# A hybrid conv and attention layer: a fifth weight group in seven products, conv taps by ScalarE and adding DMAs

## The chip, the cores and the metric

The kernel runs on one core of one Trainium2 chip. The metric is the device time of one execution in microseconds, the median of several. TensorE (PE) does matrix products, VectorE (DVE) and ScalarE (ACT) work on whole tiles, GpSimd (POOL) does small scalar work here and issues the DMAs that add to their destination, SyncE (SP) issues most other DMAs. Each engine works through its own instructions in the order in which the program issues them.

## The reference

One decoder layer on x of 512 tokens by 2048 channels, in float32:

```python
h = rms_norm(x, norm_g)
z = h @ w_in                                  # 2048 x 7168
a_val, a_glu, a_gate, q, k, v, b_gate = split(z, 7 x 1024)

u = a_val * sigmoid(a_glu)
u = causal_depthwise_conv(u, conv_w, conv_b)  # 31 taps, 1024 channels
u = silu(layer_norm(u, conv_norm_g, conv_norm_b))
y_a = (u @ conv_pw_w + conv_pw_b) * silu(a_gate)

q, k = rms_norm(q), rms_norm(k)               # per head, 16 heads of 64
o = dilated_attention_mixture(q, k, v)        # three causal patterns, mixed
y_b = o * silu(b_gate)

out = x + concat(y_a, y_b) @ w_out            # 2048 x 2048
```

## The kernel before, in words

**Units, groups, slots.** Weights come in groups of 512 output columns; a group of w_in has four *units* of 4 x 128 rows (1 MB each). The list GROUPS sets the order: four "vg" groups (value and gate of the GLU), q0, k0, v0, bg0 (half of the b-gate), q1, k1, v1, ag0, ag1, bg1, then w_out and pointwise groups ("wb", "pw", "wc", "wa"). A unit is eight *slots* of TensorE work; `clock[0]` counts slots, and everything else is placed by slot: `after(n, fn)` puts a step n slots ahead into `calendar`, and each slot first issues its due steps, then its matmuls. So the order on every engine is written out by hand through the many step constants (IN_HI, NORM, B_STEPS, WA_PARTS and so on).

**Precision.** A float32 product is made of three float16 ones: each operand is split into a high and a low part (`split_hi`/`hi` on ScalarE, `split_lo`/`lo` on VectorE), and `tri` issues high x high, high x low, low x high. The scale of a group comes from a bound on its weights: `measure` sums squares on ScalarE, `bound` adds them up through TensorE, VectorE and POOL. The first two groups are done in float32 matmuls (`exact_matmuls`), while the sums for the RMS norm of x are still being made.

**Seven products.** The groups in SEVEN (before: vg3, q0, k0, v0) use a scheme of seven half-size block products instead of eight (`input_products`): sums of weight blocks are made in place by adding DMAs on POOL's queue and one difference on VectorE, sums of x blocks are made once (`sum_x`), and the results are joined in `copy`, `joint`, `fourth` and `out`. Such a group has 28 steps instead of 32 slots. The "wa" groups of w_out use the same scheme (`seven_products`, `seven_parts`).

**The weight ring.** `raw_pool` has eight 1 MB buffers. When a unit's low part is made, its buffer is let go, the unit eight further on is loaded, and some slots later it is measured.

**Conv.** `conv` is a generator that works through channel blocks 0 to 7 in pairs. A block's 31 taps are one ScalarE instruction (with the bias) and 30 multiply-adds on VectorE, each over up to 512 tokens. `run_conv` pulls taps from it each slot while an estimate of VectorE's load lies below PACE, a number of nanoseconds for each slot. After the last pair come the sums for the layer norm, the norm itself and the split of its result into `u16`, which the "pw" units read.

**Attention.** `attention(hf)` places pairs of heads at fixed slots (`at_pair`), PERIOD slots apart: scores at 0 and 3, exps, reciprocal roots, high and low parts, a transposing DMA (`turn`), and then `values` and `put` in `end_pair`, which the next pair's `begin` calls, or the last pair's own step.

Of the kernel before, what the change touches and what calls it, by code (L numbers as in the profile page):

```python
# [19 lines left out]
P = 128  # L20
# [13 lines left out]
WARM = 9  # L34
KU = 4
PERIOD = {0: 32, 1: 32}
# [3 lines left out]
PACE_FROM = (63, 114, 169, 225, 297, 361)  # L40
PACE = [1170, 1350, 1285, 1310, 1480, 1465, 1480]
# [8 lines left out]
GROUPS = [("vg", 0), ("vg", 1), ("vg", 2), ("vg", 3), ("q", 0), ("k", 0), ("v", 0), ("bg", 0), ("q", 1), ("k", 1), ("v", 1),  # L50
# [12 lines left out]
B0_AT = -13  # L63
YB = [0, 1, 4, -2, -1, 3]
B_STEPS = [-5, 3, 20, 7]
B1_STEPS = [3, 9, 28, 6]
Y_STEPS = [5, 1]
Y_SUMS = [2, 1, 2, 1]
SPLIT_PW = [0, 2]
# [4 lines left out]
NORM = {'q': [3, 8, 8, 10, 5], 'k': [3, 7, 9, 13, 5]}  # L74
NORM_K0 = [3, 1, 10, 11, 13, 2]
WA_ADD = [{'s1': (4,), 's4': (1,), 's2': (-4,), 's3': (-8,)}, {'s1': (8, 9, 14), 's4': (2, 3, 8), 's2': (-2, -1, 4), 's3': (-10, -9, -9)}, {'s1': (8, 9, 12), 's4': (2, 3, 8), 's2': (-2, -1, 4), 's3': (-16, -15, -16)}, {'s1': (5, 6), 's4': (0, 2), 's2': (-3, -2), 's3': (-16, -15)}]
WA_PARTS = [{'a11': (-29,), 'a22': (-27,), 'a12': (-1,), 's3': (1,), 's2': (4,), 's1': (7,), 's4': (9,)}, {'a11': (-8, -7, -3), 'a22': (-4, -3, 2), 'a12': (-2, 2, 5), 's3': (4, 5, 10), 's2': (8, 9, 14), 's1': (11, 12, 17), 's4': (15, 16, 21)}, {'a11': (-7, -7, -2), 'a22': (-4, -3, 2), 'a12': (-1, 0, 5), 's3': (4, 5, 10), 's2': (8, 9, 14), 's1': (11, 12, 17), 's4': (15, 16, 21)}, {'a11': (-5, -5), 'a22': (-4, -3), 'a12': (-2, -1), 's3': (0, 1), 's2': (4, 5), 's1': (7, 8), 's4': (10, 11)}]
WA_OUT = [1, 4, 1, 5, 5, 6, 6]
MEASURE = 16
BOUND = [3, -3, 6, 5]  # L80
SPLIT_AT = [0, 3]
MEASURE_AT = [15, 9]
# [27 lines left out]
def layer(ctx: ExitStack, tc: tile.TileContext, xt, w1, w2, w3, g_in, conv_w, conv_b,  # L110
# [45 lines left out]
    A.activation(small.tile([P, 1], F32, name="warm", bufs=1), ones[:, 0:1], AF.Copy)  # L156
# [156 lines left out]
    def exact_hi(n):  # L313

        i, k = divmod(n, KU)
        wt = parts[i, k] = part_pool.tile([P, 2, S], R32, name="wr", tag="part")
        A.activation(wt[:, 0], raw[i][:, k], AF.Copy)

    def exact_lo(n):
# [3 lines left out]
        if k == KU - 1:  # L323
            raw.pop(i)
            load(i + RING)
            after(max(6, 32 - 3 * i - 5 * (8 - RING)), lambda: measure(i + RING))
# [9 lines left out]
    def split_lo(i):  # L336
        if i < n_plain:
            wh, wl = parts[i]
            V.scalar_tensor_tensor(wl, raw.pop(i), wscale[units[i][3:]][0], wh, op0=OP.mult, op1=OP.subtract)
            load(i + RING)  # L340
            after(MEASURE_AT[of_next(i) not in SEVEN], lambda: measure(i + RING))

# [15 lines left out]
    def split_x(k):  # L358
# [10 lines left out]
        A.activation(h, x, AF.Copy, scale=g)  # L369
# [97 lines left out]
    def evac_vg(g, m, ps):  # L467
# [15 lines left out]
        elif m % 2 == 0:  # L483
            t = glu[i] = temp("glu")
            if g < FIRST:
# [4 lines left out]
        else:  # L490
            t = u[i] = slot("u")
            if g < FIRST:
                V.tensor_mul(t, ps, rrow)
                V.tensor_mul(t, t, glu.pop(i))
# [99 lines left out]

    def shifted():
# [5 lines left out]
        for i in range(6):  # L601
            square(i)
            yield
            if len(squares) > 1:
                V.tensor_add(acc2[0], acc2[0], squares.pop(0))
                yield
        V.tensor_add(acc2[0], acc2[0], squares.pop(0))

    def conv():

        for i0 in range(0, 8, 2):
            while i0 + 1 not in u:
                yield 1
            for i in (i0, i0 + 1):
                cv[i] = slot("cv")
                A.activation(cv[i], u[i], AF.Identity, scale=cw[:, i, TAPS - 1:TAPS], bias=cb[:, i:i + 1])  # L616
            yield 2
            for j in range(TAPS - 2, -1, -1):
# [9 lines left out]
            elif i0 == 2:  # L628
                for i in (i0, i0 + 1):
                    nc.gpsimd.dma_start(acc, cv[i], accum_op=OP.add)  # L630
            elif i0 == 4:
                for i in (i0, i0 + 1):
                    V.tensor_add(acc, acc, cv[i])
                    yield 0
# [30 lines left out]
        for i in range(8 + 2):  # L665
# [9 lines left out]
            yield LN_STEPS[7]  # L675

# [125 lines left out]
    def two_heads(pair):  # L802
# [78 lines left out]
        for a, e in ((0, 7), (1, 11)):  # L881
            h = (13, 18)[a]
            plan += [(6, lambda a=a: shift(a)), (e + 4, lambda a=a: roots(a)), (h + 6, lambda a=a: turn(a))]
            for i in range(NT):
                plan += [(e, lambda a=a, i=i: exps(a, i))]
                plan += [(h + i // 2, lambda a=a, i=i: high(a, i)), (h + 3 + i // 2, lambda a=a, i=i: low(a, i))]
# [9 lines left out]
    def attention(hf):  # L896
        start = max(clock[0] + 28, max(at_pair.values(), default=0) + PERIOD[0])
        start += (PHASE - start) % 8
        for p4 in range(4):
            at_pair[4 * hf + p4] = start + p4 * PERIOD[hf]  # L900

            def begin(pair=4 * hf + p4):
                end_pair(pair - 1)
# [7 lines left out]
                after(PERIOD[hf] - (pair == 7), lambda: end_pair(pair))  # L911
# [104 lines left out]
    def seven_parts(g):  # L1016
# [182 lines left out]
    def input_products(i0):  # L1199
# [20 lines left out]
        def lo(name, pair):  # L1220
# [61 lines left out]
        def out(name):  # L1282
# [19 lines left out]
            elif kind == "v":  # L1302
# [5 lines left out]
                after(2, lambda: V.tensor_tensor(to[:, :, :, DH:], src, to[:, :, :, :DH], op=OP.subtract))  # L1308
            else:
# [37 lines left out]
    for k in range(2):  # L1347
        load_part(0, k, k + 1)
        fetch_x(k)
    for n in range(1, 8):  # L1350
# [6 lines left out]
    for n in range(2):  # L1357
        exact_hi(n)
        exact_lo(n)
        split_x(n)  # L1360
    exact_hi(2)
# [3 lines left out]
    def startup(n):  # L1365
# [8 lines left out]
        if n == 0:  # L1374
# [7 lines left out]
            for m in (32, 33, 36):  # L1382
# [158 lines left out]
```

## Time and profile before

| | |
|---|---|
| median of 3 runs | 811.38 us (811.3 to 811.81) |
| profiled execution | 810.59 us, span 808.8 us |
| TensorE busy | 802.1 us (99%) |
| VectorE busy | 718.1 us (89%) |
| ScalarE busy | 571.4 us (71%) |
| POOL busy | 161.2 us (20%) |
| DMA queues | SP and ACT 42.8%, POOL 15.3% of 16 engines |

The span runs from the first to the last instruction. Busy times are sums over an engine's instructions. A row of a group of instructions names line, engine, operation, output<-inputs and shapes, the count, then busy us and mean ns of one, and the idle time of the engine ahead of it with what ended it. A row of the waits has engine and instruction, what it waited for, the total, the number of times and the longest. Nearly all VectorE instructions have line 105, the helper that records their load.

### The profile page before, as it was taken

The page shows a single profiled execution, that of the slowest core. Times are in us where ns is not written, and L with a number is a line of the kernel's source. Part 1 is how long each engine was busy: PE and PEld are TensorE (multiplying, and loading weights), DVE is VectorE, ACT ScalarE, POOL GpSimd, SP SyncE. Part 2 cuts the span into 40 slices and gives each one's busy share as a digit, 9 for nine tenths or more (in the row PEclk, how much of TensorE's full clock was granted, in tenths as well). Part 3 has the DMA queues.
Part 4 walks back from the last instruction along what each step waited for, and adds up shares of the span by engine and source line. Part 5 has one row for each costly group of instructions (what it writes and reads, how often), then busy time and mean ns, then how long its engine had stood idle before and what let it go on. Part 6 is the DMA issues. An engine that isn't in the chain of part 4 may idle for free.

```text
span 808.8 us, 13884 instructions
## 1 busy us (share of the span) xinstructions
PE 802.1 (99%) x5448; PEld 518.9 (64%) x5448; DVE 718.1 (89%) x1208; ACT 571.4 (71%) x800; POOL 161.2 (20%) x165
## 2 busy tenths in 40 slices
PE   9999999999999999999999999999999999999998
PEld 6787745888888854444444444444544445888887
DVE  6668899899999989999899999899699689988884
ACT  6667775677888697757849458496799877757630
POOL 0002011313535101104113010110130012523410
PEclk9999999999999999999999999999999999999999
DMA  9852353694989846352863825426272556698551
GB/s 343 332 233 103 106 154 85 127 276 75 301 159 273 225 154 169 105 134 94 182 164 89 190 100 149 125 59 165 102 189 85 156 171 157 160 270 234 107 118 53
DMA packets 88097, 130.87 MB, mean 162 GB/s; under 512 B 62688, under 2 KB 67040, under 8 KB 78816
## 3 DMA queue, kind: packets, MB, share of 16 engines
q1 hardware_dynamic: 80544, 107.37, 42.8%
q0 software_dynamic: 7200, 22.55, 15.3%
q8 instruction: 42, 0.69, 0.3%
q14 instruction: 23, 0.19, 0.1%
q10 hardware_dynamic: 288, 0.07, 0.0%
HBM read 88.56 MB, written 4.19 MB: 115 GB/s over the span
## 4 chain that ended last, share of the span: by engine, by line
PE 88%; DVE 7%; DMA 4%; issue 1%; POOL 0%; ACT 0%; SPq 0%; POOLq 0%; ACTq 0%; DVEq 0%
PE ps_l L451 23%; PE ps_l L453 23%; PE ps_l L452 23%; PE ps_l L980 11%; DMA wf<-wf 2%; PE ps_s L826 2%; PE ps_o L867 2%; DVE y L105 2%; DVE res L105 1%; DMA wf<-w_dram 1%; PE ps_s L451 1%; PE ps_s L453 1%; PE ps_s L452 1%; DVE ws L105 1%; DVE ysum L105 1%
## 5 line engine op out<-in xcount | busy, mean ns | idle before, releaser
L105 DVE SCALAR_TENSOR_TENSOR cv<-u,cw,cv 128x511 f32<-128x511 f32 (+14 forms) x240 | 162.3, 727 | 2.7 <-ACT cv L616 2.7
L215 ACT ACTIVATE junk<-wf 128x2048 uint8<-128x2048 f32 x68 | 129.1, 1898 | 10.0 <-DMA wf<-w_dram 9.9
L451 PE MATMUL ps_l<-x,wh 128*128 128x512 f16 x320 | 121.3, 379 | 0.0
L453 PE MATMUL ps_l<-x,wl 128*128 128x512 f16 x320 | 121.3, 379 | 0.0
L452 PE MATMUL ps_l<-x,wh 128*128 128x512 f16 x320 | 121.3, 379 | 0.0
L105 DVE SCALAR_TENSOR_TENSOR ws<-wf,ws 128x1024 f16<-128x1024 f32 x84 | 107.2, 1278 | 8.0 <-ACT ws L1218 6.8
L331 ACT ACTIVATE wh<-wf,ws 128x2048 f16<-128x2048 f32 x39 | 77.7, 1993 | 25.5 <-PE ps_l L452 21.5
L105 DVE SCALAR_TENSOR_TENSOR wl<-wf,ws,wh 128x2048 f16<-128x2048 f32 x39 | 91.5, 2345 | 3.1 <-ACT wh L331 2.8
L451 PEld LDWEIGHTS <-wh 128*128 128x128 f16 x432 | 42.3, 98 | 53.1 <-issue 4.0
L453 PEld LDWEIGHTS <-wl 128*128 128x128 f16 x432 | 42.3, 98 | 51.2 <-issue 0.3
L452 PEld LDWEIGHTS <-wh 128*128 128x128 f16 x432 | 42.3, 98 | 48.5 <-issue 0.3
L451 PE MATMUL ps_l<-wh,x 128*128 128x512 f16 x192 | 72.8, 379 | 0.0
L453 PE MATMUL ps_l<-wh,x 128*128 128x512 f16 x192 | 72.8, 379 | 0.0
L452 PE MATMUL ps_l<-wl,x 128*128 128x512 f16 x192 | 72.8, 379 | 0.0
L980 PE MATMUL ps_l<-xr,wr 128*128 128x512 f32 x288 | 69.9, 398 | 0.2 <-ACT xr L369 0.2
L229 POOL TENSOR_SCALAR ws<-ws 128x1 f32<-128x1 f32 x20 | 17.6, 881 | 255.3 <-DVE ws L105 254.9
L980 PEld LDWEIGHTS ps_l<-xr,wr 128*128 128x128 f32 x288 | 54.1, 189 | 13.9 <-ACT xr L369 1.1
L1218 ACT ACTIVATE ws<-wf,ws 128x1024 f16<-128x1024 f32 x56 | 62.2, 1136 | 1.0 <-ACT ws L1218 0.4
L193 POOL TENSOR_TENSOR ss<-ss,half 128x8 f32<-128x8 f32 x16 | 35.4, 2217 | 94.6 <-DVE ss L105 94.6
L451 PE MATMUL ps_l<-ws,tx 128*128 128x256 f16 x192 | 52.3, 273 | 0.0
L453 PE MATMUL ps_l<-ws,tx 128*128 128x256 f16 x192 | 52.3, 273 | 0.0
L452 PE MATMUL ps_l<-ws,tx 128*128 128x256 f16 x192 | 52.3, 273 | 0.0
(287 smaller groups left out, 1935.2 us busy)
## 6 DMA issues: line engine op xcount, KB each, us to landing
wf<-w_dram SPq DMA_DIRECT2D x72, 1024.0 KB, 5.4
wf<-wf POOLq DMA_DIRECT2D x36, 512.0 KB, 6.0
x<-xt_dram SPq DMA_DIRECT2D x16, 256.0 KB, 6.7
res<-xt_dram SPq DMA_DIRECT2D x8, 512.0 KB, 6.3
out_dram<-res SPq DMA_DIRECT2D x15, 256.0 KB, 4.3
wf<-w_dram SPq DMA_DIRECT2D x7, 512.0 KB, 7.2
wf<-wf POOLq DMA_DIRECT2D x12, 256.0 KB, 6.9
wf<-w_dram SPq DMA_DIRECT2D x2, 256.0 KB, 3.2
```

What stands on the lines that cost most here:

```text
L105: return getattr(self.engine, name)(out, src, *args, **kw)
L193: G.tensor_tensor(ap, ap, half.to_broadcast(list(ap.shape)), op=OP.pow)
L215: A.activation(junk[:, :n], src, AF.Square, scale=scale, accum_out=acc)
L229: G.tensor_scalar(scale, scale, 1e-24 if name == "u" else 1e-30, 2.0 ** (-2 * top), op0=OP.max, op1=OP.mult)
L331: A.activation(parts[i][0], raw[i], AF.Copy, scale=wscale[units[i][3:]][0])
L451: T.matmul(ps, ah, bh, start=first, stop=False, skip_group_check=more)
L452: T.matmul(ps, ah, bl, start=False, stop=False, skip_group_check=more)
L453: T.matmul(ps, al, bh, start=False, stop=last, skip_group_check=more)
L826: T.matmul(ps[i, a], qk["q", hf][p4 // 2][rows, p4 % 2, q, i * P:w], qk["k", hf][p4 // 2][rows, p4 % 2, k, :w], start=n == 0, stop=n == 2)
L867: T.matmul(po[rows, i * P:(i + 1) * P], vs[hf][j // 2][:, j % 2, 2 * p4 + a, vp * DH:(vp + 1) * DH], got["t", a][:, pp * (ALL // P) + FROM ...
L980: T.matmul(banks[group, m], wt[:, a, m * P:(m + 1) * P], xk[b], start=k == 0 and a == b == 0, stop=k == KC - 1 and a == 1)
L1218: A.activation(t[:, 0], block(name, pair), AF.Copy, scale=wscale[group][0])
```

## The change

- ("bg", 0) moves ahead of ("q", 0) and joins SEVEN; its output branch in `input_products` writes Silu halves on ScalarE. In GROUPS the k0 group and with it the first pair of heads come four units later.
- The pairs of heads are 28 slots apart instead of 32, with their inner steps from ATT; `values` and `put` of a pair come eight slots behind the next pair's begin.
- `stage`: for channel blocks 4 and 5 one tap each, for 6 and 7 twelve taps each are made by ScalarE (a scaled copy into a temporary) and added to the block's sum by a DMA on POOL's queue. The sums `cv` of blocks 4 to 7 lie in one weight buffer, taken at slot 251 by `refill` in place of a load and given back behind the layer norm.
- Four of the sums of squares for the layer norm are adding DMAs (`add_square`).
- The start: one warm-up matmul fewer, the first weight block on ScalarE's DMA queue, the warm-up activation behind it, the first high part in two pieces, the first part of x on VectorE.
- FREE_AT: units of the last output group are measured 13 slots behind their load instead of 9; many step constants and PACE are set anew. In vg1, one value in four is first copied by ScalarE.

```diff
-WARM = 9
+WARM = 8
-PERIOD = {0: 32, 1: 32}
+PERIOD = {0: 28, 1: 28}
-PACE_FROM = (63, 114, 169, 225, 297, 361)
-PACE = [1170, 1350, 1285, 1310, 1480, 1465, 1480]
+PACE_FROM = (61, 112, 167, 222, 291, 359)
+PACE = [1080, 1350, 1285, 1310, 1540, 1420, 1495]
-GROUPS = [("vg", 0), ("vg", 1), ("vg", 2), ("vg", 3), ("q", 0), ("k", 0), ("v", 0), ("bg", 0), ("q", 1), ...
+GROUPS = [("vg", 0), ("vg", 1), ("vg", 2), ("vg", 3), ("bg", 0), ("q", 0), ("k", 0), ("v", 0), ("q", 1), ...
-SEVEN = (("vg", 3), ("q", 0), ("k", 0), ("v", 0))
+SEVEN = (("vg", 3), ("bg", 0), ("q", 0), ("k", 0), ("v", 0))
+STAGE = {4: [265, 1, 6], 6: [283, 12, 4]}
+CV_FROM = 251
+ATT = [7, 9, 11, 12, 2, 2, 5]
-SHIFT_STEP = 5
+SHIFT_STEP = 3
+VALUES = 8
+SQ_DMA = 4
+BY_ACT = (0,)
-BOUND = [3, -3, 6, 5]
+BOUND = [3, -3, 6, 6]
+FREE_AT = 13
...
+    def refill():
+        if cv_wanted[0]:
+            cv_wanted[0] = False
+            cv_raw.append(raw_pool.tile([P, KU, S], F32, name="wf"))
+            return len(units)
+        n = n_loaded[0]
+        n_loaded[0] += 1
+        load(n)
+        return n
...
-        A.activation(wt[:, 0], raw[i][:, k], AF.Copy)
+        for a, b in ((0, P), (P, S)) if n == 0 else ((0, S),):
+            A.activation(wt[:, 0, a:b], raw[i][:, k, a:b], AF.Copy)
...
-        A.activation(h, x, AF.Copy, scale=g)
+        if k:
+            A.activation(h, x, AF.Copy, scale=g)
+        else:
+            V.tensor_scalar(h, x, g, None, op0=OP.mult)
...
+    def add_square(i):
+        if i <= SQ_DMA + 1:
+            nc.gpsimd.dma_start(acc2[0], squares.pop(0), accum_op=OP.add)
+        else:
+            V.tensor_add(acc2[0], acc2[0], squares.pop(0))
...
+    def stage(i0):
+        _, taps, step = STAGE[i0]
+        for i in (i0, i0 + 1):
+            begin_cv(i, cv_raw[0][:, i - 4])
+
+        def tap(i, d):
+            t = temp("tap")
+            A.activation(t[:, d:], u[i][:, :S - d], AF.Copy, scale=cw[:, i, TAPS - 1 - d:TAPS - d])
+            after(1, lambda: nc.gpsimd.dma_start(cv[i][:, d:], t[:, d:], accum_op=OP.add))
+
+        for n in range(2 * taps):
+            after(2 + n * step, lambda n=n: tap(i0 + n % 2, 1 + n // 2))
+        after(6 + 2 * taps * step, lambda: staged.add(i0))
...
     def conv():
...
+            if i0 in STAGE:
+                while i0 not in staged:
+                    yield 1
+            else:
+                for i in (i0, i0 + 1):
+                    begin_cv(i, slot("cv"))
+                yield 2
-            for j in range(TAPS - 2, -1, -1):
+            for j in range(TAPS - 2 - (STAGE[i0][1] if i0 in STAGE else 0), -1, -1):
...
+        def last_of_cv():
+            cv_raw.clear()
+            n = refill()
+            after(9, lambda: measure(n))
+        after(3, last_of_cv)
...
-        for a, e in ((0, 7), (1, 11)):
-            h = (13, 18)[a]
-            plan += [(6, lambda a=a: shift(a)), (e + 4, lambda a=a: roots(a)), (h + 6, lambda a=a: turn(a))]
+        for a in range(2):
+            e, h = ATT[a], ATT[2 + a]
+            plan += [(ATT[0] - 1, lambda a=a: shift(a)), (e + ATT[4], lambda a=a: roots(a)), (h + ATT[6], lambda a=a: turn(a))]
...
-                end_pair(pair - 1)
-                after(PERIOD[hf] - (pair == 7), lambda: end_pair(pair))
+                after(PERIOD[hf] + (VALUES if pair < 7 else -1), lambda: end_pair(pair))
...
-                after(9, lambda: measure(i + RING))
+                after(FREE_AT if units[i + RING][4] == 3 else 9, lambda: measure(i + RING))
...
+            elif kind == "bg":
+                for m in range(2):
+                    i = 4 * g + 2 * x + m
...
+                    A.activation(u_part["bg", i][:, z * H:(z + 1) * H], pair[:, m], AF.Silu)
...
-        load_part(0, k, k + 1)
+        load_part(0, k, k + 1, nc.sync if k else nc.scalar)
         fetch_x(k)
+    A.activation(small.tile([P, 1], F32, name="warm", bufs=1), ones[:, 0:1], AF.Copy)
```

More of the change, by code (lines that the diff above doesn't have):

```diff
@@ L324, in exact_lo @@
             raw.pop(i)
-            load(i + RING)
-            after(max(6, 32 - 3 * i - 5 * (8 - RING)), lambda: measure(i + RING))
+            n_next = refill()
+            after(max(6, 32 - 3 * i - 5 * (8 - RING)), lambda: measure(n_next))
     def split_hi(i):
@@ L339, in split_lo @@
             V.scalar_tensor_tensor(wl, raw.pop(i), wscale[units[i][3:]][0], wh, op0=OP.mult, op1=OP.subtract)
-            load(i + RING)
-            after(MEASURE_AT[of_next(i) not in SEVEN], lambda: measure(i + RING))
+            n_next = refill()
+            after(MEASURE_AT[of_next(i) not in SEVEN], lambda: measure(n_next))
     def split16(src, scale, name):
@@ L484, in evac_vg @@
             t = glu[i] = temp("glu")
-            if g < FIRST:
+            if g < FIRST and m in BY_ACT:
+                A.activation(t, ps, AF.Copy)
+                after(GLU_AT[0], lambda: V.tensor_mul(t, t, rrow))
+                after(GLU_AT[1], lambda: A.activation(t, t, AF.Sigmoid))
+            elif g < FIRST:
                 V.tensor_mul(t, ps, rrow)
@@ L604, in shifted, with begin_cv @@
             if len(squares) > 1:
-                V.tensor_add(acc2[0], acc2[0], squares.pop(0))
+                add_square(i)
                 yield
-        V.tensor_add(acc2[0], acc2[0], squares.pop(0))
+        add_square(6)
+    staged = set()
+    def begin_cv(i, t):
+        cv[i] = t
+        A.activation(cv[i], u[i], AF.Identity, scale=cw[:, i, TAPS - 1:TAPS], bias=cb[:, i:i + 1])
+    def stage(i0):
[9 more added lines that the diff above has]
+        after(6 + 2 * taps * step, lambda: staged.add(i0))
+    calendar.setdefault(CV_FROM, []).append(lambda: cv_wanted.__setitem__(0, True))
+    for i0, at in STAGE.items():
+        calendar.setdefault(at[0], []).append(lambda i0=i0: stage(i0))
     def conv():
@@ L1308, in out @@
                 after(2, lambda: V.tensor_tensor(to[:, :, :, DH:], src, to[:, :, :, :DH], op=OP.subtract))
+            elif kind == "bg":
+                for m in range(2):
+                    i = 4 * g + 2 * x + m
+                    if ("bg", i) not in u_part:
+                        u_part["bg", i] = slot("gate")
+                    A.activation(u_part["bg", i][:, z * H:(z + 1) * H], pair[:, m], AF.Silu)
+                    halves["bg", i] = halves.get(("bg", i), 0) + 1
+                    if halves["bg", i] == 2:
+                        bg[i] = u_part.pop(("bg", i))
+                        after(1, lambda i=i: gate_o(i))
             else:
@@ L1358, in layer @@
         exact_hi(n)
-        exact_lo(n)
+        if n:
+            exact_lo(n)
         split_x(n)
+        if not n:
+            exact_lo(n)
     exact_hi(2)
@@ L1454, in layer @@
             need = KU * units[i][2] + KU - 1
-            while need not in u16:
-                next(convolution)
+            for _ in range(200):
+                if need not in u16:
+                    next(convolution)
         for n, (m, hf) in enumerate(order):
```

58 lines of the change are left out of this document (29 added, 29 removed).

## The prediction, made before the changed kernel ran

> **What bounds the kernel now.** I read the page's span and busy rows first, then who waited on TensorE, then TensorE's busy time by stretches.
>
> ```profile
> span 808.8 us, 13884 instructions
> PE 802.1 (99%) x5448; PEld 518.9 (64%) x5448; DVE 718.1 (89%) x1208; ACT 571.4 (71%) x800; POOL 161.2 (20%) x165
> PE   9999999999999999999999999999999999999998
> ```
>
> The profiled execution took 810.59 us, 1.8 around its span and 0.8 under the median of 811.38. TensorE is busy in every slice. A busy TensorE need not be a dense one, so the waits come next:
>
> ```profile
> PE ps_l L451 <- ACT wsd L1053: 1.0, 1, 1.0
> PE ps_s L227 <- ACT junk L215: 0.8, 1, 0.8
> PE ps_l L453 <- DVE wsd L105: 0.4, 1, 0.4
> ```
>
> TensorE waits little over 2 us for other engines in the whole span. What is left to shorten is its number of matmuls, its start, these stalls, and the 3.4 us behind its last matmul. Two stretches hold one group of columns each: the group ahead of the first seven-product group, and that first one (columns: length, then each engine's busy time and instructions, clock, DMA share, GB/s). The third runs from the plain b-gate group to the layer norm.
>
> ```profile
> 96.75:138.23 41.48, 41.48 (x195) 18.82 (x195) 39.63 (x66) 27.48 (x35) 4.48 (x6) 1.00 0.39 114
> 138.23:174.83 36.60, 36.60 (x338) 32.81 (x337) 33.78 (x46) 25.03 (x30) 9.21 (x10) 1.00 0.77 203
> 328.00:565.00 237.00, 237.00 (x1428) 110.83 (x1425) 227.11 (x415) 162.04 (x242) 36.69 (x30) 1.00 0.50 133
> ```
>
> A plain group is 16 row blocks x 4 x 3 = 192 matmuls of 512 columns: 41.48/192 = 0.216 us each. A seven-product group is 7 x 2 x 2 x 4 x 3 = 336 of 256 columns: 36.60/336 = 0.109. (The few matmuls over these counts are tiny sums.) Both are dense, at the full granted clock (1.00). VectorE has 9 us free in 237 of the third stretch; it is the engine that could become the bound.
>
> **The change, part by part.**
>
> *A fifth group in seven products.* ("bg", 0) turns from plain to seven products and moves ahead of ("q", 0). TensorE: 41.48 − 36.60 = −4.9 us, on the path throughout, since nothing else sets its pace. Every group behind q0, k0, v0 keeps its slot number. The cost lies on the other engines:
>
> ```profile
> L105 DVE SCALAR_TENSOR_TENSOR ws<-wf,ws 128x1024 f16<-128x1024 f32 x84 | 107.2, 1278 | 8.0 <-ACT ws L1218 6.8 <-ACT ws L1053 1.1
> L105 DVE SCALAR_TENSOR_TENSOR wl<-wf,ws,wh 128x2048 f16<-128x2048 f32 x39 | 91.5, 2345 | 3.1 <-ACT wh L331 2.8
> L331 ACT ACTIVATE wh<-wf,ws 128x2048 f16<-128x2048 f32 x39 | 77.7, 1993 | 25.5 <-PE ps_l L452 21.5 <-DVE ws L105 3.8
> L1218 ACT ACTIVATE ws<-wf,ws 128x1024 f16<-128x1024 f32 x56 | 62.2, 1136 | 1.0 <-ACT ws L1218 0.4 <-PE ps_l L452 0.3 <-PE ps_l L453 0.3
> L105 DVE TENSOR_TENSOR wf<-wf 128x1024 f32<-128x1024 f32 x12 | 14.6, 1216 | 0.0
> L105 DVE SCALAR_TENSOR_TENSOR cb<-ps_l,esc,cb 128x512 f32<-128x512 f32 x6 | 4.5, 745 | 0.0
> L1268 ACT ACTIVATE cb<-ps_l,esc 128x512 f32<-128x512 f32 x9 | 6.1, 679 | 7.6 <-PE ps_l L453 7.1 <-POOL esc L464 0.6
> L1214 POOL DMA_DIRECT2D wf<-wf x24 | 21.5, 1008 | 62.2 <-ACT ws L1218 30.7 <-DVE ws L105 25.4 <-DVE u L105 2.8
> ```
>
> VectorE: 14 low halves x 1.278 + 2 differences x 1.216 + 4 joins at 0.745 at most − 4 plain low halves x 2.345 = 17.9 + 2.4 + 3.0 − 9.4 = +13.9. ScalarE: 14 x 1.136 − 4 x 1.993 + 5 copies x 0.679 = +11.3, and eight half-width Silus for four whole ones, between nothing and +2.7 (each half at the price of a whole copy). POOL: 6 more adding DMAs x 1.0 = +6. The stretch of the first such group has 2.8 us of VectorE free although it is full of conv taps, and conv can wait, so I take this as hidden.
>
> *26 taps, the adds, the squares.* Channel blocks 4 and 5 get one tap each, 6 and 7 twelve each, as a scaled copy on ScalarE and an adding DMA on POOL's queue. Four sums of squares become adding DMAs too.
>
> ```profile
> L105 DVE SCALAR_TENSOR_TENSOR cv<-u,cw,cv 128x511 f32<-128x511 f32 (+14 forms) x240 | 162.3, 727 | 2.7 <-ACT cv L616 2.7
> L105 DVE TENSOR_TENSOR lnacc<-lnacc,lnsq x7: 680/685/693, 517.5 to 570.4; 128x512 f32<-128x512 f32 x7
> L346 ACT ACTIVATE u<-cv,us x8: 705/707/710, 597.7 to 618.2; 128x512 f16<-128x512 f32 x8
> L630 POOL DMA_DIRECT2D lnacc<-cv x2: 866/902/937, 386.1 to 391.9; - x2
> DMA to landing us min/median/max: 4.3/4.7/5.1
> ```
>
> VectorE: −26 x 0.727 − 4 x 0.685 = −21.6. ScalarE: +26 x 0.707 = +18.4. POOL: 30 x 0.9 = +27. With the group, and one x part moved from ScalarE to VectorE at the start (±0.7), VectorE goes from 718 to about 711, ScalarE from 571 to about 602, POOL from 161 to about 194. None of these is a time of its own; over a span that shrinks by some 7, VectorE's free time stays as it is, 90 us. Twelve adds go into the same tile at distances of eight slots (8 x 6 x 0.216 = 10.4 us) and land in 4.3 to 5.1, so each waits for nothing.
>
> *A weight buffer for conv sums.* The ring has seven buffers for some 200 slots, so a unit is loaded 8 slots (10.4 us) later. Before, the last unit of a plain group is loaded 45 slots ahead of the group, measured nine slots (11.7 us) on, and the group's scale is ready at −25, 17 slots ahead of the first split at −8; now nine of these go (one by the bound's later step). Cost zero; without that cover ScalarE would wait inside a measurement, which is the 1.75 us stall priced below.
>
> *Pairs of heads every 28 slots instead of 32.* No instruction more, and the same two interruptions of TensorE a pair. Pair 0 now starts at slot 250 instead of 218, pair 7 at 446 instead of 450. So about one pair more falls into the stretch 328 to 565, where taps and squares went. In it, exps to reciprocals has two slots instead of four:
>
> ```profile
> L839 ACT ACTIVATE sx<-sx,st,sc 128x512 f32<-128x512 f32 x16 | 12.8, 801 | 0.0
> L105 DVE SCALAR_TENSOR_TENSOR hl<-sx,st,hl 128x512 f16<-128x512 f32 x16 | 11.9, 745 | 0.0
> L105 DVE CUSTOM_DVE_ANT_0 sx<-ps_s,tab 128x512 f32<-128x512 f32 x16 | 10.4, 686 | 4.2 <-PE ps_s L826 4.2
> ```
>
> A pair costs VectorE, with widths 512, 384, 256, 128 in proportion, 2 x 2.5 x (0.745 + 0.686) = 7.2 us. Four exps of a head take 2.5 x 0.801 = 2.0 us and their four sums at most as much again, against two slots of 2.6: VectorE may wait up to 1.4 us, 16 times, 22 us at the worst. In the stretch that is +7.2 and between 0 and +22, against −21.6: between −14 and +8. Behind it lies the layer norm, whose last block is ready here:
>
> ```profile
> L105 DVE SCALAR_TENSOR_TENSOR u<-cv,us,u x8: 730/743/768, 598.5 to 624.2; 128x512 f16<-128x512 f32 x8
> L451 PE MATMUL ps_l<-u,wh x64: 376/379/389, 618.9 to 661.6; 128*128 128x512 f16 x64
> ```
>
> The second pointwise unit begins 48 matmuls after 618.9, at 629.2, so the last block has 4.3 us of cover. I take the term as zero: the waits fall on the engine that has been in front, as ScalarE has a third of the stretch free.
>
> *The start.* One warm-up matmul fewer; the first weight block goes out on ScalarE's queue while SP issues x first; the first high part is cut in two; x's first part is made by VectorE.
>
> ```profile
> 0.98 4.02 PE L171 MATMUL ps_s<-wz 128*128 128x512 f16 x9 [0.98 <-POOL wz L168]
> 1.19 0.42 SPq L356 DMA_DIRECT2D x<-xt_dram  x1
> 3.68 0.63 ACT L317 ACTIVATE wr<-wf 128x512 fp32r<-128x512 f32 x1 [1.03 <-DMA wf<-w_dram]
> 4.41 0.72 ACT L369 ACTIVATE xr<-x,gcol 128x512 fp32r<-128x512 f32 x1
> 5.19 3.09 PE L980 MATMUL ps_l<-xr,wr 128*128 128x512 f32 x10 [0.18 <-ACT xr L369]
> 5.19 34.26 PE ps_l L980 x144
> ```
>
> x goes out 0.46 earlier; weights, behind the gcol DMA, some 0.4 later, at about 4.1 instead of 3.68. A quarter of its copy, then the first matmul: 4.4 to 4.6 instead of 5.19, so −0.6 to −0.8 at the front. The warm-up matmuls run 4.02/9 = 0.44 apart, twice the later 0.216 (half the rate), and the first ten real ones take 3.09, where ten at the mean of the first 144 (34.26/144 = 0.238, from the chain of waits) would take 2.4; so the early matmuls still run slowly and the earlier start buys slow ones. I take −0.5 (0 to −0.8). The Trainium skill (TensorE: Matmul & The Clock Gate, "Part 1: The HAM clock gate") says that TensorE runs at half clock until it has been busy for about 3.4 us, in a window that does not start with the kernel. By that rule the release stays where it is and a start 0.7 earlier gains about half, 0.35; the trace's half-rate spacing agrees, the moment of release is not shown in the rows above.
>
> *A later measurement in the last stage.* FREE_AT = 13 puts the measuring of a last-group unit 13 slots behind its load instead of 9. Here is what stalls TensorE now:
>
> ```profile
> 738.26 1.91 ACT L215 ACTIVATE junk<-wf 128x2048 uint8<-128x2048 f32 x1 [3.91 <-DMA wf<-w_dram]
> 741.90 1.91 ACT L215 ACTIVATE junk<-wf 128x2048 uint8<-128x2048 f32 x1 [1.02 <-DMA wf<-w_dram]
> 743.81 0.70 ACT L1053 ACTIVATE wsd<-wf,wjs 128x512 f16<-128x512 f32 x1
> 743.27 0.27 PE L453 MATMUL ps_l<-y,wsc 128*128 128x256 f16 x1
> 744.57 0.28 PE L451 MATMUL ps_l<-y,wsd 128*128 128x256 f16 x1 [1.02 <-ACT wsd L1053]
> 745.36 0.28 PE L453 MATMUL ps_l<-y,wsd 128*128 128x256 f16 x1 [0.40 <-DVE wsd L105]
> ```
>
> ScalarE sits 4.9 us in front of two measurements whose weights have not landed, and the high part wsd that TensorE needs is queued behind them. TensorE's starts are 1.30 and 0.67 apart where 0.109 is due: 1.19 + 0.56 = 1.75. By the plans, the two measurements move from slots −3 and −2 of the third output group to +1 and +2, behind that wsd at −2; the next part behind them is wanted four slots (5.2 us) later, against 1.9 for a measurement. I take −1.6 (0 to −1.75). The 0.8 wait for the last squares (L227) stays: its chain is unchanged.
>
> *The sum.* −4.9 − 0.5 − 1.6, and +0.3 for new small stalls (0 to +5, of which I take the low end, since TensorE's waits for VectorE were 0.4 in all): −6.7. From 810.6 that is 803.9; from the median, 804.7.
>
> **The rivals.**
>
> *Part of the gain is eaten, about 807.7.* VectorE loses time to ScalarE's exps as above, conv ends late, and the pointwise product waits. At the worst of the bound (+8) less the 4.3 of cover it is 3.7, less what conv's own pacing recovers: about 3 late, 804.7 + 3 = 807.7. For it: 227 of 237 us busy. Against: the middle of −14 to +8 is below zero.
>
> *Slower, about 820.* The chain of twelve adds into one tile decides. POOL waits for each landing, and VectorE's own taps on that tile wait for the last. With landings over the spacing of 10.4 the chain grows by twelve times the excess, and at 12 us by 19; past the 4.3 of cover TensorE stands for 15, and gains of 6.7 leave 8.3: 811.4 + 8.3 = 819.7; break-even is at a landing of 10.4 + (6.7 + 4.3)/12 = 11.3. For it: one POOL wait of 11.0 on such a landing.
>
> ```profile
> POOL wf L1040 <- DMA wf<-wf: 21.4, 4, 11.0
> ```
>
> Against: that was twice the size, in the crowded last stage; the stretch in question has a DMA share of 0.50.
>
> *Better, about 803.2:* the start gains 0.8, both stalls go, no new one.
>
> *No change:* the shorter ring makes ScalarE wait for weights, as at 738, and four stalls of 1.75 give 7 back: 811.5. Against: 17 slots of cover less nine.
>
> **How the numbers follow.** Forecast 0.62 (803.9 to 806), partly eaten 0.22 (806 to 809.7), better 0.06, no change 0.05, slower 0.05. 0.2% (1.6 us) is about what a measurement here tells from no change: faster 0.90, same 0.05, slower 0.05. The range, 803.0 to 808.0, holds the forecast, the better case and most of the eaten one.
>
> **What would show it.** The b-gate's stretch on TensorE is 36.6 long and holds 336 matmuls of 256 columns (first step); the first real matmul starts at 4.4 to 4.6; no wait of TensorE for wsd; conv taps 214 on VectorE, its sum near 711, ScalarE's near 602, POOL's near 194; adding DMAs of 256 KB landing in 4 to 6. Wrong would be a TensorE wait list that adds up to several us: for u16 ahead of the pointwise units (conv late), for wh in the region with the smaller ring (weights late), or VectorE waiting on ScalarE's sx.

## The result: slower by 0.7%, and the profile after

The changed kernel takes 816.54 us (median of 8 executions, 813.1 to 820.61) against 810.71 for the kernel before (8 executions beside them, 808.52 to 811.81): a ratio of 1.0073, with a 95% interval of 1.0052 to 1.0093. 804.7 was forecast. The profiled execution took 813.1 with a span of 811.2; it is the quickest of the eight, so what the others lose beyond it is not in this trace. The top of its page, and from its chain the shares by engine:

```profile
span 811.2 us, 14333 instructions
PE 799.1 (99%) x5591; PEld 531.5 (66%) x5591; DVE 712.8 (88%) x1195; ACT 594.8 (73%) x845; POOL 196.5 (24%) x202
PE   9999999999999999999998999999999999999998
PE 75%; DVE 14%; ACT 4%; DMA 4%; issue 2%; ACTq 0%; SPq 0%; DVEq 0%
```

The busy sums came out as forecast (711, 602 and 194 for VectorE, ScalarE and POOL), and the time did not. One slice of TensorE that was 9 is now 8 (the 22nd of 40, 426 to 446 us), and VectorE has 14% of the chain where it had 7%. Who waits on TensorE, over the whole span:

```profile
PE ps_l L479 <- DVE wl L115: 2.6, 3, 1.6
PE ps_s L898 <- DVE st L115: 1.7, 3, 0.8
PE ps_l L478 <- ACT sq L586: 1.6, 2, 0.8
PE ps_l L1051 <- ACT wr L341: 1.0, 1, 1.0
```

The waits for wsd of before are gone; new are 5.9 us for low parts (wl), for reciprocals (st) and for squares (sq). By stages (columns: length, then each engine's busy time and instructions, clock, DMA share, GB/s): the plain group vg2, the seven-product groups vg3 and b0, and the plain groups q1, k1 and v1, first after, then the last of these before:

```profile
96.80:138.30 41.50, 41.50 (x195) 18.83 (x195) 39.47 (x66) 26.61 (x33) 4.47 (x6) 1.00 0.38 112
138.30:174.95 36.65, 36.65 (x338) 32.82 (x337) 33.84 (x46) 25.08 (x30) 9.20 (x10) 1.00 0.77 204
174.95:211.70 36.75, 36.75 (x340) 32.89 (x339) 33.80 (x42) 28.60 (x34) 7.82 (x11) 1.00 0.67 170
324.00:468.00 144.00, 138.13 (x834) 63.46 (x833) 131.92 (x258) 115.01 (x190) 44.80 (x38) 1.00 0.76 163
```

```profile
332.40:466.40 134.00, 134.00 (x809) 62.96 (x808) 129.89 (x231) 92.12 (x141) 26.86 (x22) 1.00 0.56 141
```

The b-gate group took 36.75, 4.75 less than a plain group. In q1 to v1 TensorE stood for 144.00 − 138.13 = 5.9 us, where before it never stood, while VectorE had 144.00 − 131.92 = 12.1 us free and ScalarE 29.0. No engine is full there. So the stretch is held by order, and the waits between 324 and 470 say in which (us in total, times, longest):

```profile
POOL wf L661 <- ACT tap L660: 52.0, 9, 35.7
...
POOL wf L661 <- DMA wf<-tap: 13.2, 2, 6.7
...
DVE st L115 <- ACT sx L911: 6.3, 6, 2.0
ACT wh L355 <- DVE ws L115: 6.2, 1, 6.2
ACT qhl L563 <- DMA wf<-tap: 6.1, 1, 6.1
ACT qhl L563 <- DVE z L115: 6.1, 1, 6.1
...
ACT sq L586 <- DMA wf<-tap: 2.9, 1, 2.9
...
ACT tap L660 <- DMA wf<-tap: 1.5, 2, 1.0
```

ScalarE waits 10.5 us for adding DMAs to land, 9.0 of them in front of instructions (qhl, sq) that have nothing to do with the conv. What they share with the taps is their place in SBUF: a tap's product, a square and the tile qhl itself are temporaries out of one pool of four (`tmp`), and a tap's temporary is not free when ScalarE has written it but when its add has landed. How long that is, all 26 taps:

```profile
L661 POOL DMA_DIRECT2D wf<-tap x26: 850/881/1206, 347.9 to 508.4; - x26
  ACT tap L660: 71.6, 15
  DMA wf<-tap: 18.0, 5
DMA to landing us min/median/max: 3.3/4.8/9.8
```

The median agrees with the 4.3 to 5.1 of before, the longest is twice that. The Trainium skill (DMA: Bandwidth & Descriptors, "Anatomy of one DMA — SWDGE (gpsimd) path") fits a DMA issued by GpSimd with 2.0 us plus its bytes at 436,000 a microsecond, an estimate of 2.6 us for these 256 KB. This trace has no landing as short.

One such wait can be followed to TensorE, in the timeline of all engines from 416 to 434 (start, length, engine, in brackets the idle time before it):

```profile
416.13 0.69 ACT L586 ACTIVATE sq<-ps_l,esc 128x512 f32<-128x512 f32 x1 [2.85 <-DMA wf<-tap]
416.55 0.87 POOL L661 DMA_DIRECT2D wf<-tap  x1 [6.54 <-DMA wf<-tap]
...
420.00 0.17 DVE L115 TENSOR_SCALAR st<-st 128x4 f32<-128x4 f32 x1 [2.01 <-ACT sx L911]
...
425.01 0.38 PE L478 MATMUL ps_l<-wh,x 128*128 128x512 f16 x1 [0.83 <-ACT sq L586]
...
428.51 0.38 PE L478 MATMUL ps_l<-wh,x 128*128 128x512 f16 x1 [0.75 <-ACT sq L586]
...
430.71 2.35 DVE L115 SCALAR_TENSOR_TENSOR wl<-wf,ws,wh 128x2048 f16<-128x2048 f32 x1
...
433.11 0.38 PE L479 MATMUL ps_l<-wl,x 128*128 128x512 f16 x1 [1.64 <-DVE wl L115]
```

ScalarE's square waits for a temporary that an add in flight still reads, and POOL waits for a landing too, 6.54 us. The exps behind that square on ScalarE come late, VectorE stands 2.01 us for them, and VectorE's next low part wl starts only at 430.71. TensorE waits three times, 3.2 us together. That each of these three waits goes back to this square is read from the order of the rows; the runs below test it. With the 0.80 that it waits for st at 402.26 that is 4.0.

### The profile page after: what moved, and what is told of

Read it like the earlier page. It is cut to its first block, busy times and chain, and to the rows that moved or that the text cites. A ratio compares the mean times of both kernels' runs of the same rounds, so it can differ in the third digit from the quotient of the medians.

```text
span 811.2 us, 14333 instructions
## 1 busy us (share of the span) xinstructions
PE 799.1 (99%) x5591; PEld 531.5 (66%) x5591; DVE 712.8 (88%) x1195; ACT 594.8 (73%) x845; POOL 196.5 (24%) x202
## 4 chain that ended last, share of the span: by engine, by line
PE 75%; DVE 14%; ACT 4%; DMA 4%; issue 2%; ACTq 0%; SPq 0%; DVEq 0%
PE ps_l L478 19%; PE ps_l L479 18%; PE ps_l L480 18%; PE ps_l L1051 11%; DVE wl L115 3%; DVE cv L115 3%; PE ps_s L478 2%; PE ps_s L480 2%; PE ps_s L479 2%; DMA pt<-hl 2%; ACT sx L911 2%; DVE ws L115 1%; DMA qk<-qhl 1%; PE ps_o L939 1%; DVE sx L115 1%
## 5 line engine op out<-in xcount | busy, mean ns | idle before, releaser
L115 DVE SCALAR_TENSOR_TENSOR ws<-wf,ws 128x1024 f16<-128x1024 f32 x98 | 125.3, 1280 | 8.0 <-ACT ws L1289 6.7
L478 PE MATMUL ps_l<-x,wh 128*128 128x512 f16 x256 | 97.2, 380 | 0.0
L479 PE MATMUL ps_l<-x,wh 128*128 128x512 f16 x256 | 97.1, 379 | 0.0
L480 PE MATMUL ps_l<-x,wl 128*128 128x512 f16 x256 | 97.1, 379 | 0.0
L115 DVE SCALAR_TENSOR_TENSOR wl<-wf,ws,wh 128x2048 f16<-128x2048 f32 x35 | 82.1, 2346 | 3.3 <-ACT wh L355 3.3
L355 ACT ACTIVATE wh<-wf,ws 128x2048 f16<-128x2048 f32 x35 | 69.8, 1993 | 18.4 <-PE ps_l L479 10.2
L115 DVE SCALAR_TENSOR_TENSOR cv<-u,cw,cv 128x511 f32<-128x511 f32 (+29 forms) x120 | 82.0, 730 | 0.0
L1289 ACT ACTIVATE ws<-wf,ws 128x1024 f16<-128x1024 f32 x70 | 77.7, 1136 | 1.7 <-DMA wf<-wf 0.4
L478 PEld LDWEIGHTS <-wh 128*128 128x128 f16 x368 | 36.0, 98 | 45.7 <-issue 3.6
L480 PEld LDWEIGHTS <-wl 128*128 128x128 f16 x368 | 35.9, 98 | 44.0 <-DVE wl L115 0.7
L115 DVE SCALAR_TENSOR_TENSOR wf<-u,cw,wf 128x499 f32<-128x499 f32 (+28 forms) x94 | 63.1, 727 | 0.5 <-DMA wf<-tap 0.5
L1051 PEld LDWEIGHTS ps_l<-xr,wr 128*128 128x128 f32 x288 | 53.8, 188 | 14.7 <-ACT wr L341 2.1
L479 PEld LDWEIGHTS <-wh 128*128 128x128 f16 x368 | 36.0, 98 | 40.5 <-issue 0.3
```

The source lines that it names most:

```text
L115: return getattr(self.engine, name)(out, src, *args, **kw)
L355: A.activation(parts[i][0], raw[i], AF.Copy, scale=wscale[units[i][3:]][0])
L478: T.matmul(ps, ah, bh, start=first, stop=False, skip_group_check=more)
L479: T.matmul(ps, ah, bl, start=False, stop=False, skip_group_check=more)
L480: T.matmul(ps, al, bh, start=False, stop=last, skip_group_check=more)
L1051: T.matmul(banks[group, m], wt[:, a, m * P:(m + 1) * P], xk[b], start=k == 0 and a == b == 0, stop=k == KC - 1 and a == 1)
```

## The experiments

The expectations set theories against each other, by letters. **H** and **T**: the adding DMAs are the cause, in their first form because each holds a temporary until it lands. **C**: the same for whatever buffer the product lies in, as ScalarE stands in front of a tap until the buffer's last add has landed. **Q**: POOL's queue, standing for ScalarE's taps, is the cause. **M**: the adds' traffic is, by sharing the DMA engines. **V**: VectorE has become the bound. **P**: the new pace of the conv leaves VectorE with a backlog. All ratios are against the kernel before, run beside each kernel.

**The adds left out, and the adds without held temporaries**

```diff
 no_add      - after(1, lambda: nc.gpsimd.dma_start(cv[i][:, d:], t[:, d:], accum_op=OP.add))
             + pass
 add_from_u  + after(1, lambda: nc.gpsimd.dma_start(cv[i][:, d:], u[i][:, :S - d], accum_op=OP.add))
```

> The changed kernel with ScalarE's 26 scaled copies, but without the 26 adding DMAs: these taps are left out of the conv. A temporary is free as soon as ScalarE has written it, POOL issues nothing for it, and no add shares the DMA engines with the transposes. Theory H (the adding DMAs are the cause, through the temporary that each holds, through POOL's queue or through the DMA engines): the stalls between 324 and 468 us fall from 8 to under 3, 806 to 810 us. Theory V (VectorE has become the bound: with pairs every 28 slots it has more to do and to wait for in this stretch than TensorE's shorter time leaves): VectorE's work is the same, so the stalls stay, 813 to 819 us.

> The same 26 copies and 26 adding DMAs of the same size into the same sums, but each DMA reads the unscaled block u instead of the copy (the taps' weights are left out): no temporary is held until a DMA lands, the DMA traffic and POOL's queue are as in the changed kernel. If the held temporaries are what hurts (theory H, first form): as without adds, 806 to 810 us. If POOL's queue or the DMA engines hurt (theory H, other forms), or theory V: 813 to 819 us.

no_add: 808.27, ratio 0.9998 (0.9971 to 1.0026). add_from_u: 810.81, 1.0017 (0.9992 to 1.0042), with the same DMAs, the same bytes and ScalarE's 26 products still made. So the loss hangs neither on ScalarE's work nor on the traffic, and theory M falls. The waits in the same stretch of add_from_u, and then TensorE's in its whole span:

```profile
ACT junk L224 <- DMA wf<-w_dram: 16.2, 5, 6.6
...
ACT qhl L563 <- DVE z L115: 4.4, 2, 3.0
...
DVE st L115 <- ACT sx L911: 3.0, 3, 1.1
```

```profile
PE ps_l L479 <- DVE wl L115: 0.9, 2, 0.7
PE ps_s L898 <- DVE st L115: 0.9, 2, 0.5
```

No wait of ScalarE for an add is left, VectorE's for sx halves, and of TensorE's 5.9 us for wl, st and sq 1.8 remain: the four waits of 4.0 us told above are not there. Its last matmul starts at 802.8, after's at 807.8. The 1.8 lie between 345 and 383 us, and no_add, without any of the 26 adds, has the same four waits there: they are not the adds' doing.

Two couplings are cut at once in add_from_u: the temporary is not held, and POOL's queue, with the reciprocal roots in it, no longer stands for ScalarE's tap. One more kernel brings the second back alone:

```diff
 pool_wait   + G.tensor_scalar(small.tile([P, 1], F32, name="tw", bufs=2), t[:, d:d + 1], 1.0, None, op0=OP.mult)
             + nc.gpsimd.dma_start(cv[i][:, d:], u[i][:, :S - d], accum_op=OP.add)
```

> As add_from_u (the 26 adding DMAs read u instead of ScalarE's product, so no temporary is held until an add lands), and with a one-column POOL instruction on each of ScalarE's 26 products ahead of its adding DMA: POOL, and the reciprocal roots queued behind it, stand for ScalarE as in the changed kernel. Left out: the tap's weight in 26 of the conv's adds. Theory H (the held temporaries are the cause): as add_from_u, 808 to 811, and no wait of ScalarE for an adding DMA. Theory Q (POOL's queue standing behind ScalarE's products is the cause): about 816, with POOL waiting some 50 us for ScalarE's taps between 324 and 470 and TensorE losing 6 us or more between 320 and 440.

> add_from_u again, beside pool_wait and on the same chip, so that the two stand side by side: 808 to 811 by both theories. Left out: the tap's weight in 26 of the conv's adds.

pool_wait: 811.1, 1.0023 (1.0001 to 1.0045). add_from_u2: 812.56, 1.0036 (1.0011 to 1.0061), 1.6 us above the top of what was expected of it; its interval just overlaps the changed kernel's (1.0052 to 1.0093), pool_wait's does not. The longest waits in pool_wait, 324 to 470:

```profile
POOL tw L663 <- ACT tap L660: 53.5, 6, 35.5
...
POOL wf L664 <- DMA wf<-u: 13.0, 3, 6.7
...
ACT wh L355 <- DVE ws L115: 6.3, 1, 6.3
ACT junk L224 <- DMA wf<-w_dram: 5.9, 3, 4.1
ACT qhl L563 <- DVE z L115: 5.5, 1, 5.5
```

POOL stands 53.5 us for ScalarE's taps, as in after (52.0), and 13.0 for landings, as in after (13.2), yet ScalarE waits for no add, and the time is add_from_u's. (In add_from_u POOL stands as long, 30.4 us for VectorE and 28.5 for landings.) Theory H, the held temporaries, stands; theory Q, POOL's queue, falls.

**Less work for VectorE, another pace, later roots**

```diff
 less_conv   - for j in range(TAPS - 2 - (STAGE[i0][1] if i0 in STAGE else 0), -1, -1):
             + for j in range(TAPS - 2 - (STAGE[i0][1] if i0 in STAGE else 0), -1 if i0 in STAGE else 4, -1):
 pace        - PACE = [1080, 1350, 1285, 1310, 1540, 1420, 1495]
             + PACE = [1080, 1350, 1285, 1310, 1400, 1420, 1495]
 roots       - ATT = [7, 9, 11, 12, 2, 2, 5]
             + ATT = [7, 9, 11, 13, 4, 2, 5]
```

> The last five taps of channel blocks 0 to 3 are left out: 20 of 214 multiply-adds on VectorE, 12 to 14 us of its work; ScalarE's taps, their DMAs and the pairs are as in the changed kernel. Theory V: VectorE's backlog in 324 to 468 us shrinks by that much, the stalls there fall under 3 us, 805 to 810 us. Theory H: the held temporaries and the adds are the same, most of the stalls behind 380 us stay, 812 to 817 us.

> One number: the pace of conv in slots 222 to 291 is 1400 ns a slot instead of 1540. Theory P: VectorE's run of 12 taps in a row ahead of a low part at 345 us is cut up, the ScalarE wait of 6 us for the scale goes, and with it most stalls between 344 and 432 us; 807 to 811 us. Theory T: the stalls behind 380 us stay, since the temporaries are held as before; 813 to 819 us.

> The reciprocals of a pair's sums come four slots behind its exps, as in the kernel before, instead of two; the second head's high parts one slot later; pairs stay 28 slots apart. Theory V in the form that VectorE's waits for ScalarE's exps (6.3 us in the stretch 324 to 470) are what tips it: these waits go under 2 us, and the time falls by 3 to 6 us, 810 to 813 us. Theory H: no more than 1 us of change, 814 to 818 us.

All three end above both ranges that were expected of them. less_conv: 822.5, 1.0157 (1.0129 to 1.0185). With 20 multiply-adds of VectorE fewer it is no quicker, so theory V falls; why it is 6 us slower than the changed kernel stays open. Waits from 324 to 470:

```profile
DVE st L115 <- ACT sx L911: 9.2, 6, 2.7
...
ACT qhl L563 <- DMA wf<-tap: 6.2, 1, 6.2
```

The wait for an add is there again, and VectorE's for sx has grown. pace: 826.9, 1.0209 (1.0191 to 1.0227): with fewer conv steps per slot the gaps of TensorE from 360 to 440 stay (7.1 us, after 6.4), and those from 600 to 640 grow from 1.3 to 11.5, where it waits for parts that come late behind the layer norm. Theory P falls. roots: 820.76, 1.0141 (1.0107 to 1.0176); ScalarE's waits for adds under qhl grew to 11.6.

**Another home for the temporaries**

```diff
 slot_taps   - t = temp("tap")
             + t = slot("tap")
 two_slabs   - STAGE = {4: [265, 1, 6], 6: [283, 12, 4]}
             + STAGE = {6: [283, 12, 4]}
             + t = cv_raw[0][:, i - 6]
 two_start   two_slabs with the start of the kernel before
 two_wide    two_slabs with
             + STAGE = {6: [267, 10, 6]}
             + CV_FROM = 235
 ring6       + t = cv_raw[1][:, len(taps_done) % 4]    (a second weight buffer, the ring at six)
```

> The taps' products lie in the large pool of 35 tiles instead of the four temporaries that squares, norm parts and taps share; nothing else changes. Theory T (the temporaries run out: a tap holds one until its adding DMA has landed, and ScalarE stands in front of the next square or norm part): TensorE's stalls between 324 and 468 us, 7 us in the profiled run of the changed kernel, fall below 2, no ScalarE wait for a tap's DMA is left, 806 to 809 us. Theory P (VectorE has a backlog of conv taps in slots 222 to 291, since the pace there went up to 1540 ns a slot, so scales, score reads and low parts come late): the stalls stay, 813 to 820 us.

> The whole layer is computed. The sums of channel blocks 4 and 5 go back to ordinary tiles and their one tap each back to VectorE; in the weight buffer their two slabs hold the taps' products of blocks 6 and 7, one slab each, so 24 adding DMAs stay and none holds one of the four shared temporaries. Theory H, first form (held temporaries): like the kernel whose adds held none, so 806 to 811 us, with the stalls between 360 and 440 us at 2 us instead of 6. If POOL's queue and the DMA engines were as much of it: 812 us or more.

> The same, and the start of the kernel before: nine warm-up matmuls, the first weight block on SP's queue ahead of x, the warm-up activation ahead of the loads (x's first part stays on VectorE and the first high part in two pieces). In the profiles so far the float32 stage ends at 96.6 to 98.7 us with the new start and at 96.8 and 97.4 with the old: 0.3 to 1.5 us less than two_slabs, 805 to 809.5 us, if the new start costs that; the same time if it does not.

> As two_slabs (the taps' products of blocks 6 and 7 in one slab each of the weight buffer), but ten taps each instead of twelve, six slots apart instead of four, from slot 267: a slab has 12 slots (15.6 us) until its next tap instead of 8 (10.4 us). VectorE gets four taps more (some 3 us). Theory C (ScalarE, which works in order, stands in front of a tap until the buffer's last adding DMA has landed; in two_slabs it stood 15.5 us for that, so giving the taps a place of their own did not uncouple them): ScalarE's wait for these DMAs falls under 4 us, the stalls between 360 and 440 us under 4, 808 to 812 us. Theory M (the adds themselves, by sharing the DMA engines with the transposes of q, k and the heads' parts, hurt whatever ScalarE does): 814 to 819 us.

> The changed kernel with a second weight buffer taken from slot 243 until the taps are done: its four slabs hold the taps' products in turn, so a slab is wanted again 16 slots (20 us) later, and the four shared temporaries are left to squares and norm parts. For that time the ring has six buffers instead of seven. Theory C: ScalarE does not wait for adds any more, the stalls between 360 and 440 us go to 2, 807 to 811 us, unless weights now come late (a ScalarE wait for weights then shows it, and TensorE waits for high parts). Theory M: 814 to 819 us with ScalarE not waiting for adds.

None of these helps, and none comes into the range of theory H or T, or of C: slot_taps 818.16 (1.0101, 1.0078 to 1.0124), two_slabs 818.15 (1.011, 1.0085 to 1.0134), two_start 818.32 (1.0114, 1.0083 to 1.0144), two_wide 828.73 (1.022, 1.0199 to 1.0241), ring6 818.85 (1.0098, 1.0075 to 1.0121). From ScalarE's waits between 324 and 470, for each of slot_taps, two_slabs, two_wide and ring6 in turn (of two_wide only the wait for an add):

```profile
ACT tap L660 <- DMA wf<-tap: 17.9, 3, 6.7
```

```profile
ACT wf L660 <- DMA wf<-wf: 15.5, 3, 6.6
```

```profile
...
ACT wf L660 <- DMA wf<-wf: 1.9, 1, 1.9
```

```profile
ACT wh L355 <- DVE ws L115: 12.2, 3, 7.9
ACT qhl L563 <- DVE z L115: 9.1, 2, 7.8
ACT junk L224 <- DMA wf<-w_dram: 6.8, 4, 4.1
```

In slot_taps the tap itself waits until the add of an earlier tap has landed; in two_slabs each block has one slab, and the tap waits for its predecessor. Fewer taps further apart (two_wide) cut that from 15.5 to 1.9 us, as C said, but the last conv tap then starts at 574.5 instead of 561.4, and TensorE loses some 17 us more than in the changed kernel around the layer norm (summed over the gaps between its matmuls from 560 to 720). In ring6 no wait for an add is left, and others have grown with the smaller ring: for a group's scale (ws, 12.2 us where after has 6.2), for z (9.1, after 6.1) and for weights (6.8, after 2.1). By their own forecasts two_slabs and ring6 speak for the adds' traffic (theory M). Against M stand add_from_u and pool_wait, with as many adds of the same size or two more, and quicker by 5 us or more. So these five runs don't confirm the held temporaries by a repair; a home that costs nothing was not found.

**No taps on ScalarE**

```diff
 no_taps     + STAGE = {4: [265, 0, 6], 6: [283, 0, 4]}
```

> All 26 taps go back to VectorE (19 us of work); the conv sums stay in the weight buffer, the order of groups and the pairs stay. Theory T: the adding DMAs and the held temporaries were the cause, so the stalls in 324 to 468 us go, and VectorE's 19 us come back as a later conv: the layer norm may be late by some us, 806 to 812. Theory P: VectorE has more to do, the backlog stays or grows, 815 to 825 us.

831.21, 1.026 (1.0223 to 1.0297). TensorE's waits in the whole span:

```profile
PE ps_l L478 <- ACT u L370: 6.0, 1, 6.0
PE ps_l L479 <- DVE u L115: 3.0, 3, 1.4
PE ps_s L454 <- DVE lnacc L115: 2.7, 1, 2.7
PE ps_l L479 <- DVE ws L115: 2.3, 3, 1.1
PE ps_l L478 <- ACT ws L1289: 1.3, 1, 1.3
```

The time lies above both ranges. TensorE stands 0.9 us from 360 to 440, where after has 4.8, but the last conv tap starts at 594.4, and TensorE waits at the layer norm. There the granted clock is at 0.50 for 17 us in three pieces between 606.5 and 657.7, which is part of the loss. The taps cost some 5 us through the temporaries, and without them the time is 14.7 longer (831.21 − 816.54): with the pairs of heads at 28 slots and this conv pace they are needed.

**The start, and the last stage, alone in the kernel before**

```diff
 b_start     + WARM = 8; load_part(0, k, k + 1, nc.sync if k else nc.scalar); first high part in two pieces; x part 0 by VectorE
 b_free      + after(13 if units[i + RING][4] == 3 else 9, lambda: measure(i + RING))
```

> The kernel before with the change's start alone: one warm-up matmul fewer, the first weight block on ScalarE's queue behind gcol, its high part in two pieces, x's first part by VectorE. The prediction's term: -0.5 (0 to -0.8). By the traces of the kernels with this start the first weight block reaches ScalarE some 1 us later than from SP, so the first matmul starts at 5.5 instead of 5.2, and now and then the clock is released 2 us later: 0 to +1.5 against the kernel before.

> The kernel before with one edit: units of the last output group are measured 13 slots behind their load instead of 9. Both theories: the stall of 1.75 us at 743 us goes as it did in the changed kernel, nothing else moves: 1.5 to 1.9 us under the kernel before, about 809 us.

b_free: 808.88, 0.9985 (0.9972 to 0.9998). The stall at 743 us is gone and nothing new has come in that stage. It is quicker than the kernel before by 0.15%, with an interval that just excludes no change, and is quicker than the changed kernel. b_start: 810.54, 1.0009 (0.9997 to 1.0021), between −0.2 and +1.7 us. Its first microseconds:

```profile
1.15 0.47 ACTq L292 DMA_DIRECT2D wf<-w_dram  x1
...
5.18 1.24 ACT L317 ACTIVATE wr<-wf 128x128 fp32r<-128x128 f32 x3 [2.03 <-DMA wf<-w_dram]
5.54 2.07 PE L983 MATMUL ps_l<-xr,wr 128*128 128x512 f32 x4 [0.96 <-ACT wr L317]
```

The first weight block, issued on ScalarE's queue at 1.15, reaches ScalarE at 5.18, 4.0 us later; it had been forecast for 4.1. So the first matmul starts at 5.54, where the kernel before has 5.19, and TensorE, with one warm-up matmul fewer, now stands 0.96 us ahead of it, where it stood 0.18. In this trace the first nine real matmuls start 0.43 apart; in the profile before only the first three are that slow. The float32 stage ends at 98.24 in this trace, 1.5 us later than before; but the stall at 743 us, untouched by the edit, is 0.40 us here instead of 1.75, so that the last matmul starts only 0.2 later. two_start, two_slabs with most of the old start, ended where two_slabs did (818.32 and 818.15).

## Why the prediction was wrong

**Wrong: the adds that "wait for nothing", and VectorE's term taken as zero.** The step asked whether an add waits for the one before it, and priced that by the sum's tile alone (landing 4.3 to 5.1 against a distance of 10.4 us). It did not ask what the add's source holds. The product stays in one of four shared temporaries until its add has landed, up to 9.8 us, and ScalarE, which works in order, stands in front of other work for it. The range of −14 to +8 for the stretch had VectorE's work in mind; the wait was ScalarE's. Even the tile's part failed: late taps bunch up the adds, and POOL waited 18.0 us in 5 places for landings.

**Wrong: +0.3 for new small stalls.** TensorE's last matmul starts 2.4 us later than before (807.8 against 805.4), where −6.7 was forecast: 9.1 are missing. The group gave 4.8 and the last stage 2.0, so the stretch from q1 to the layer norm lost 9.2. The held temporaries are some 4.5 to 5.0 of it: add_from_u's last matmul is 5.0 earlier (802.8 against 807.8), and 4.5 of that is gained between 383 and 615 us, a stretch with most of the taps' adds. The other 4.2 to 4.7 are there without them too. 1.8 are TensorE's waits for wl and st from 345 to 383, the rest is in gaps that were not taken apart, and the cause of both stays open: the pairs at 28 slots, the shorter times inside a pair and the new pace were never run alone in the kernel before. These losses are of the kind that the range of 0 to +5 named, and the low end was taken because before had few of them; but before had no taps on ScalarE and fewer heads in that stretch.

**Wrong: the start, −0.5.** Measured alone, −0.2 to +1.7. The failed step is "at about 4.1" for the first weights, which came at 5.18 in b_start. The end of the float32 stage shows no gain either: 96.75 before, 96.8 after. In 14 profiles with the new start the matmuls come at the slow spacing up to about 6.3 us in nine, and up to 8.9 to 9.9 in five, which then end the stage some 1.5 us later; the three with the old start are all of the first kind. The Trainium skill (TensorE: Matmul & The Clock Gate, "Part 1: The HAM clock gate") has a window of about 3.4 us that runs freely, so that the release falls differently from run to run; the two moments, some 3 us apart, agree with that. That the gap of 0.96 us ahead of the first matmul causes the later one was not tested.

**Right:** −4.9 for the group (4.75 in its stage; it was not run alone); −1.6 for the last stage (2.0 in its stage, −0.15% in b_free); the busy sums of the engines; the smaller ring at no cost in the profiled execution, as no wait for weights is among TensorE's. Two small slips of the working change nothing: VectorE's free time in the third stretch is 9.9 us, not 9, and the rival of no change adds up to 811.7, not 811.5.

**The rival that ended on the other side** had the right place and the wrong mechanism: it let POOL and VectorE's own taps wait for a chain of adds into one tile, with a break-even at landings of 11.3 us. The longest landing was 9.8, and by that rival the change should have won.

**Open.** The executions of after reach from 813.1 to 820.61, and those of no_add, add_from_u and pool_wait from 807 to 818, where before's stay within 5 us. Three things on record are part of it. The later full rate at the start accounts for some 1.5. Then, with the very program of after up to the first tap at 347 us, TensorE stands between 296 and 318, in the seven-product group v0, 3.4 us in the profile of slot_taps, 3.7 in that of no_taps (the last two of its rows shown above), 0.9 in add_from_u2 and not at all in after and add_from_u. So the cost of the fifth group on the other engines, which the prediction took as hidden, is not hidden in every execution; ScalarE waits in that stage for adding DMAs of weight blocks (3.6 us in no_taps) and for weights (4.0 in slot_taps); which of these decides was not taken apart. Last, the granted clock is 0.996 to 0.998 in three of after's eight executions, which is 1.6 to 3.3 us at this length; but those of 817.33 and 817.72 us had it at 1.0. What they lost is in no profile.

## What to carry to other kernels

When work is moved to an asynchronous add, count how long its source stays occupied, not only whether the adds wait for each other: a shared pool of temporaries turns a DMA's slowest landing into a wait of an in-order engine, in front of whatever takes the next buffer. Equal or lower busy sums say nothing of that; ask who hands each buffer back, and when. And measure the small, separable parts alone. Of the two that were measured so here, the one-line change in the last stage paid and the start did not; the fifth group, which gave 4.75 us in its stage, would have been the next to try.

## What the runs showed of the hardware

DMA transposes of qk took longer to land in the changed kernel: 3.3 us in the median (2.4 to 9.9) before, 6.2 (2.4 to 11.7) after. The taps' adds are the smaller part of that, as the median is 5.0 in no_add, without them. In add_from_u, where the time comes back, it is 6.0: slow transposes alone did not cost the time. And POOL's standing 53 us for another engine, with small but urgent work behind it, cost nothing that could be measured.

A stall of TensorE can cost more than its own length, because the granted clock may fall behind it. In two_slabs TensorE stood 2.31 us up to 421.43 and 1.71 up to 423.51 (columns as in the stages above; the clock is the number behind the engines):

```profile
418.00:421.90 3.90, 1.50 (x7) 0.49 (x5) 1.03 (x3) 3.90 (x13) 0.87 (x1) 1.00 0.47 82
421.90:428.70 6.80, 5.19 (x13) 1.89 (x13) 6.08 (x12) 6.80 (x16) 2.45 (x2) 0.50 0.52 168
```

The clock was at half for 6.8 us. In pace it was at half for 3.4 us from 403.4, behind a stall of 3.24 that ended at 402.54; in less_conv for 3.4 from 392.2, behind one of 3.12 that ended at 391.08. In after (longest stall 1.64) and roots (2.60) it stayed at 1.00.
